# Dilated attention on one Trainium2 core: affine rows through SyncE, merges used later, a longer projection lead, and the last merge behind five evictions

## The chip, the cores and the metric

The kernel runs on one core of a Trainium2 chip. The core has a matrix engine (PE, with a separate row PEld for its weight loads), a vector engine (DVE), a scalar engine (ACT), a general engine (POOL) and a sequencer that only issues transfers (SP, also called SyncE). Each engine carries out its own list of instructions strictly in order, and they meet through semaphores. DMA transfers are issued by SP or by POOL here, in the order of that engine's list; an instruction at the head of a list that has to wait holds up everything behind it on its engine.

The metric is the device time of one execution in microseconds (us), the median of several.

## The reference

The program is a decoder trunk of two layers on 1024 tokens of width 1024, all in float32. Layer 0 mixes tokens with a gated MLP, layer 1 with dilated attention; each is followed by a squared-ReLU MLP. The change touches the attention layer only.

```python
def mixer_b(h, w_qkv, w_out, slopes):
    qkv = (h @ w_qkv).reshape(B, S, N_PAT, 3, B_HEADS, B_HEAD_DIM)
    outs, lses = [], []
    for g, (window, dilation) in enumerate(B_PATTERNS):      # (128, 1), (512, 4), (2048, 16)
        o, lse = dilated_branch(qkv[:, :, g, 0], qkv[:, :, g, 1], qkv[:, :, g, 2], window, dilation, slopes)
        outs.append(o)
        lses.append(lse)
    wts = jax.nn.softmax(jnp.stack(lses, axis=0), axis=0)[..., None]
    o = jnp.sum(wts * jnp.stack(outs, axis=0), axis=0)
    return o.reshape(B, S, B_HEADS * B_HEAD_DIM) @ w_out
...
    y = mixer_b(h, b_w_qkv[j], b_w_out[j], slopes)
    x = layer_norm(ALPHA * x + gate * y, ln_g[i, 0], ln_b[i, 0])
```

There are 16 heads of 64 and three dilations. Each dilation gives an output and a log-sum-exp; the three outputs are then mixed with softmax weights over the dilations. That mixing is called a merge below.

## The kernel before

A float32 product is made of three matmuls: each operand is split into a high part (`hi`, a cast by ACT) and a low part (`lo`, a subtraction by DVE), and hi x hi, hi x lo and lo x hi are summed. Every name that ends in `hi` or `lo` is such a part, and both are made in `split` (lines 102 and 103). So nearly every result of PE passes through ACT and then DVE before PE can use it again.

The attention stage works through 24 groups: eight pairs of heads, `hp` 0 to 7, times three dilations g = 2, 1, 0. Each group has eight slots with two half slots each. `at(slot, half)` enters a piece of work in a table; the loop at the end of `attention` runs through the slots, issues the pieces of each half slot and then one or two steps of `project()`. A step is three matmuls of 128x512 of the query and key projections of dilations 1 and 2 (`psq`, `psk`; 512 steps in all); those are spread between the attention work so that PE has something to do while DVE and ACT work on scores and probabilities. Before the first slot 44 steps are issued as a lead. From the written list a scheduler makes the order of each engine: it may move an instruction past others of its engine as long as the data allow, except for those that are given to `tc.keep_in_program_order`.

Four parts matter for the change.

*Affine rows.* The residual of the later normalisation needs ALPHA * (x * ln_g + ln_b). Eight rows of 128 tokens (`aff_0` to `aff_7`) are loaded from `spill`, multiplied by `aff_g`, increased by `aff_b` (both scaled by ALPHA on ACT), and stored back. Loads and stores are all issued by POOL. The row buffers come from `row_bc`, a ring of three buffers that the merges' `bc` use too; `aff_g` and `aff_b` hold two of them, so the rows share the third.

*Merges.* `merge(hp)` runs while the next pair is computed; its `base` is the first slot after the pair. `read` fetches the statistics, `factors` computes weights (`mm`, `ma`, `mal`: small operations of DVE and one exponential on ACT) and stores them to `w_dram` with three transfers, `spread` reads them back, broadcast over 64 partitions each, into `bc` for g = 1, 2, 0 with two transfers each, all on SP. Then twelve pieces follow on DVE: six `scale` (line 1593, output times weight), four `add` (line 1597) and two `cut` (line 103, a split). A name such as `bc_2_1` is pair 2, dilation 1; `oT_2_1` is the output of that pair and dilation, `pTlo_5_0_3` the low part of transposed probabilities of head 5, dilation 0, piece 3, `wk_4_1_lo` and `klo_3_1` the low parts of a key weight and of projected keys (pair, dilation).

*Output projection.* `accumulate` is the product with `w_out`, in parts a to e (`psoa` to `psoe` in the traces), over k = 0 to 7, one k for each pair. Parts a and b (k 0 to 3) run inside the slots of the last groups; c (second half of the tokens, rows 4 to 7, k 2 and 3) and d (first half, rows 0 to 3, k 4 to 7, which need the later merges) run after the slots, in `go_on`. Their results are added to `acc` by DVE (line 1730); a result holds one PSUM bank until that is done.

*Weights of the output projection.* `staged_unit(k, load, gate, ready)` loads rows of `w_out` (`wo_k_raw`), multiplies them by the gate on DVE and splits them into `wo_k_hi` and `wo_k_lo`. Units 6 and 7 are split late, in `go_on`.

## Time and profile before

| | us |
|---|---|
| median of three runs | 2799.32 (2795.46 to 2805.48) |
| the profiled execution | 2804.96 |
| its span in the trace | 2803.2 |
| PE busy | 2690.2 (96%) |
| PE weight loads busy | 2216.5 (79%) |
| DVE busy | 1992.5 (71%) |
| ACT busy | 1376.3 (49%) |
| POOL busy | 99.6 (4%) |

Times in the trace count from the start of the span. The attention stage with its output projection lies at about 1377 to 2155 us. In a timeline, a row gives start, duration, engine, line, operation, output and inputs, how often, and in brackets the idle time of the engine just before it with what ended it. The mean granted clock of PE was 0.983 of full over the profiled execution. A busy PE at a lower clock takes longer for the same matmuls, so both its idle time and its clock count.

### The profile page before, as it was taken

To read this page: it belongs to the slowest core of one execution; us is meant where nothing else is said; L and a number is where in the kernel's file an instruction comes from. 1 tells how busy PE (TensorE), PEld (TensorE's weight loads), DVE (VectorE), ACT (ScalarE), POOL (GpSimd) and SP (SyncE) were. 2 spreads that over 40 slices of the span, in tenths; PEclk is the share of its full clock that TensorE was granted. 3 is DMA by queue.
4 is the path that set the end of the run, shared out by engine and by line. 5 is a ranking of instruction groups with operands and counts; after the bars stand their busy time and mean duration, and the time that the engine had idled before them with its cause. 6 is when DMAs were issued, how large, how long until landed. Compare 5 with 4: busy or idle time off the path is not lost. (4 is left out here: it accounts for less than half of the span.)

```text
span 2803.2 us, 36881 instructions
## 1 busy us (share of the span) xinstructions
PE 2690.2 (96%) x13242; PEld 2216.5 (79%) x13242; DVE 1992.5 (71%) x3594; ACT 1376.3 (49%) x2593; POOL 99.6 (4%) x171
## 2 busy tenths in 40 slices
PE   6999999999999999999997999999998999999998
PEld 5787888787888788888776877777886878888887
DVE  6777697877977696656456666666667975668887
ACT  3354475555443454334344555555663755554332
POOL 1000000000000001111100000000010000000000
PEclk9999999999999999999998999999999999999999
DMA  7543347668746446655535454445574464486562
GB/s 256 161 126 121 113 152 228 214 227 284 278 155 194 154 144 225 208 197 188 177 124 167 120 142 116 117 123 151 142 195 127 162 210 151 161 283 213 170 200 88
DMA packets 332573, 487.99 MB, mean 174 GB/s; under 512 B 50988, under 2 KB 176340, under 8 KB 332388
## 3 DMA queue, kind: packets, MB, share of 16 engines
q1 hardware_dynamic: 317124, 430.04, 48.7%
q0 software_dynamic: 15264, 55.58, 5.5%
q8 instruction: 104, 1.70, 0.3%
q14 instruction: 81, 0.66, 0.1%
HBM read 357.01 MB, written 128.53 MB: 173 GB/s over the span
## 5 line engine op out<-in xcount | busy, mean ns | idle before, releaser
L796 PE MATMUL psua<-right,left 128*128 128x512 f32 x1536 | 364.9, 391 | 0.3
L955 PE MATMUL psd<-rhi,lhi 128*128 128x512 f32 x896 | 349.8, 390 | 3.0 <-ACT part L827 3.0
L955 PE MATMUL psd<-rlo,lhi 128*128 128x512 f32 x896 | 349.4, 390 | 0.2
L955 PE MATMUL psd<-rhi,llo 128*128 128x512 f32 x896 | 348.9, 389 | 0.0
L796 PEld LDWEIGHTS psua<-right,left 128*128 128x128 f32 x1536 | 288.2, 188 | 62.1 <-DVE right L103 1.4
L1447 ACT ACTIVATE p<-p,stat 128x128 f32<-128x128 f32 (+1 forms) x384 | 168.2, 439 | 127.9 <-DVE stat L1445 127.9
L955 PEld LDWEIGHTS psd<-rhi,lhi 128*128 128x128 f32 x896 | 168.5, 188 | 39.0 <-ACT part L827 3.9
L955 PEld LDWEIGHTS psd<-rlo,lhi 128*128 128x128 f32 x896 | 168.5, 188 | 35.6 <-DVE rlo L103 1.1
L955 PEld LDWEIGHTS psd<-rhi,llo 128*128 128x128 f32 x896 | 168.5, 188 | 35.2
L796 PE MATMUL psuc<-right,left 128*128 128x512 f32 x768 | 187.2, 390 | 0.0
L128 DVE SCALAR_TENSOR_TENSOR adaacc<-adaw,silu_c,adaacc 128x512 f32<-128x512 f32 x168 | 128.5, 775 | 57.9 <-DMA adaw<-in_ada_w_dram 57.2
L796 PEld LDWEIGHTS psuc<-right,left 128*128 128x128 f32 x768 | 143.5, 188 | 30.0 <-DVE right L103 0.4
L103 DVE TENSOR_TENSOR pTlo<-pT,pThi 128x512 fp32r<-128x512 f32 (+1 forms) x160 | 99.0, 620 | 65.4 <-ACT pThi L102 64.4
L103 DVE TENSOR_TENSOR left<-ws,left 128x512 fp32r<-128x512 f32 x128 | 87.8, 687 | 71.2 <-ACT left L102 69.4
L103 DVE TENSOR_TENSOR llo<-lraw,lhi 128x1024 fp32r<-128x1024 f32 x112 | 136.4, 1218 | 0.6 <-ACT lhi L102 0.6
L1345 PE MATMUL psk<-form_L,wk_hi 128*128 128x512 f32 x384 | 136.6, 435 | 0.0
L1345 PE MATMUL psq<-form_L,wq_hi 128*128 128x512 f32 x384 | 131.9, 425 | 0.0
L102 ACT CAST left<-ws 128x512 fp32r<-128x512 f32 x128 | 79.1, 620 | 99.7 <-DVE ws L717 87.7
L1445 DVE CUSTOM_DVE_ANT_0 p<-sc,bias 128x128 f32<-128x128 f32 (+1 forms) x384 | 110.1, 345 | 17.0 <-PE sc L1431 16.0
L1499 PE MATMUL pv<-pTlo,v 128*128 128x128 f32 (+1 forms) x400 | 97.3, 286 | 25.6 <-DVE pTlo L103 25.1
L1257 PE MATMUL psv<-vrhi,form_S 128*128 128x512 f32 x384 | 120.0, 390 | 0.8 <-ACT vrhi L102 0.5
L102 ACT CAST lhi<-lraw 128x1024 fp32r<-128x1024 f32 x112 | 117.4, 1048 | 3.7 <-PE psua L796 3.6
(329 smaller groups left out, 6098.6 us busy)
## 6 DMA issues: line engine op xcount, KB each, us to landing
lraw<-forms SPq DMA_DIRECT2D x112, 512.0 KB
adaw<-in_ada_w_dram SPq DMA_DIRECT2D x192, 256.0 KB
up<-in_mlp_w_up_dram SPq DMA_DIRECT2D x64, 512.0 KB
forms<-s SPq DMA_DIRECT2D x128, 256.0 KB
rraw<-in_mlp_w_down_dram SPq DMA_DIRECT2D x64, 512.0 KB
forms<-part SPq DMA_DIRECT2D x96, 256.0 KB
v<-vs POOLq DMA_DIRECT2D x48, 512.0 KB, 3.8
vraw<-in_b_w_qkv_dram SPq DMA_DIRECT2D x42, 512.0 KB
```

Source lines behind the costliest of these rows:

```text
L102: first = A.copy(hi, src) if hi_engine is A else hi_engine.tensor_copy(hi, src)
L103: return first, lo_engine.tensor_tensor(lo, src, hi, op=ALU.subtract)
L128: ins = V.scalar_tensor_tensor(acc[:], raw[:], silu_c[:, k : k + 1], acc[:], ALU.mult, ALU.add)
L796: T.matmul(acc, w[:, a, k, :], right[p][:, b, k, :], start=p in (1, 2, 5) and k + a + b == 0, stop=k == 3 and a == 1, skip_group_check=True)
L955: ins = T.matmul(sums[kind, m][:], l[a][:, k, m * P : (m + 1) * P], r[b][:, k, :], start=p in (1, 5, 2, 3) and kp + k + a + b == 0, stop=k ...
L1257: T.matmul(acc, rows[:, m * P : (m + 1) * P], cols_, start=p in (1, 2, 5) and kp + k + a + b == 0, stop=kp == 1 and k == 1 and a == 1, ski ...
L1345: T.matmul(p[:], wu[a][:, k * P : (k + 1) * P], h_op(k, half, b), start=k + c_ == 0, stop=k == KD - 1 and c_ == 2)
L1445: V.tensor_tensor_reduce(out=pr, in0=banks[e][:, sl], in1=st["bias"][:, width - w :], scale=-0.125, scalar=3e38, op0=ALU.add, op1=ALU.min, ...
L1447: A.activation(pr, pr, AF.Exp, bias=nm, scale=-1.0, accum_out=l)
L1499: T.matmul(pvs[b][:, q0 % HALF : q0 % HALF + w_], stt, x_[:, o_ : o_ + w_], start=not begun[b], stop=left[b] == 0, skip_group_check=True)
```

## The change

It has four parts, all in `attention`.

1. The affine loads are issued by SP. `aff_g`, `aff_b` and rows 0 to 3 are loaded during the lead (steps 16 to 19 of it), rows 0 to 3 into buffers of the ring `oT`; rows 4 to 7 still use `row_bc`, with the load of row i written in slot 5i - 15 and its use in slot 5i - 12. The scaling of `aff_g` and `aff_b` on ACT is a piece of its own. The loads are no longer kept in program order. The stores stay on POOL.
2. For pairs 0 to 6 `factors` and `spread` move one slot later, and the twelve pieces start at half slot 16 instead of 12, two slots later. For the last pair `spread` moves half a slot forward.
3. The lead has 48 steps instead of 44, and the remaining steps are paced evenly over all half slots.
4. The last merge's pieces are taken out of the slots. `go_on` issues part c of the output projection first and, from its sixth step on, one merge piece behind each step; then come units 6 and 7, the rest of the merge and part d. The pieces run half by half, and part d goes through k in the groups (4, 5, 6), (7) instead of in pairs. The units 4 to 7 are made ready earlier.

```diff
-                @at(*((base + 3, 0) if hp < N_PAIRS - 1 else (base + 1, 0)))
+                @at(*((base + 4, 0) if hp < N_PAIRS - 1 else (base + 1, 0)))
                 def factors():
...
-                @at(*((base + 3, 1) if hp < N_PAIRS - 1 else (base + 1, 1)))
+                @at(*((base + 4, 1) if hp < N_PAIRS - 1 else (base + 1, 0)))
                 def spread():
...
-                steps = [lambda f=f, g=g, half=half: f(g, half) for f, g in ((scale, 2), (scale, 1), (scale, 0), (add, 2), (add, 1), (cut, 0)) for half in range(2)]
+                pieces = ((scale, 2), (scale, 1), (scale, 0), (add, 2), (add, 1), (cut, 0))
+                if hp == N_PAIRS - 1:
+                    ending["merge"] = [lambda f=f, g=g, half=half: f(g, half) for half in range(2) for f, g in pieces]
+                    return
+                steps = [lambda f=f, g=g, half=half: f(g, half) for f, g in pieces for half in range(2)]
                 pace = 2 if hp < N_PAIRS - 2 else 1
                 for n, f in enumerate(steps):
-                    n = pace * n + 12 if hp < N_PAIRS - 1 else n // 2 + 8
+                    n = pace * n + 16
                     at(base + n // 2, n % 2)(f)
...
                         affine[n] = row_bc(f"aff_{n}")
-                        tc.keep_in_program_order(nc.gpsimd.dma_start(affine[n][:], src[0, 1].partition_broadcast(P)))
-                        A.mul(affine[n][:], affine[n][:], ALPHA)
-                affine["row"] = row_bc(f"aff_{i}")
-                tc.keep_in_program_order(nc.gpsimd.dma_start(affine["row"][:], spill[1][i * P : (i + 1) * P, :]))
+                        nc.sync.dma_start(affine[n][:], src[0, 1].partition_broadcast(P))
+                t = affine[i] = vec.tile([P, S], F32, name=f"aff_{i}", tag="oT", bufs=4) if i < 4 else row_bc(f"aff_{i}")
+                nc.sync.dma_start(t[:], spill[1][i * P : (i + 1) * P, :])
+
+            def affine_scale():
+                for n in "gb":
+                    A.mul(affine[n][:], affine[n][:], ALPHA)
             def affine_row(i):
-                t = affine["row"]
+                t = affine[i]
                 for n, op in (("g", ALU.mult), ("b", ALU.add)):
...
+            at(0, 0)(affine_scale)
             for i in range(NT):
-                at(2 + 3 * i, 0)(lambda i=i: affine_load(i))
-                at(3 + 3 * i, 1)(lambda i=i: affine_row(i))
+                if i > 3:
+                    at(5 * i - 15, 0)(lambda i=i: affine_load(i))
+                at(*((i + 1, 1) if i < 4 else (5 * i - 12, 1)))(lambda i=i: affine_row(i))
...
             staged_unit(3, (-10, 1), (-9, 1), (-8, 0))
-            staged_unit(4, (-2, 0), (2, 0), (12, 0))
-            staged_unit(5, (-1, 0), (4, 0), (12, 1))
-            late = [staged_unit(6, (13, 0), (14, 1), None), staged_unit(7, (13, 1), (15, 1), None)]
+            staged_unit(4, (-2, 0), (2, 0), (8, 0))
+            staged_unit(5, (-1, 0), (4, 0), (8, 1))
+            late = [staged_unit(6, (9, 0), (11, 1), None), staged_unit(7, (9, 1), (12, 1), None)]
...
                     sums = {key: bank("mm", f"pso{name}_{key[0]}_{key[1]}") for key in groups}
-                    todo = [ks[n : n + 2] for n in range(0, len(ks), 2)]
+                    todo = ks if side > 1 else [ks[n : n + 2] for n in range(0, len(ks), 2)]
                     for pair in todo:
...
                                     T.matmul(sums[i, dh][:], ending["oT"][half][a][:, k, o : o + P], ending["units"][k][b][:, w],
-                                             start=k == ks[0] and a + b == 0, stop=k == ks[-1] and a == 1)
+                                             start=k == todo[0][0] and a + b == 0, stop=k == todo[-1][-1] and a == 1)
                             if pair is not todo[-1]:
...
             def go_on():
+                steps = ending["merge"]
+                for n, _ in enumerate(accumulate(1, range(2, 4), name="c")):
+                    if n > 4:
+                        steps.pop(0)()
                 for f in late:
                     f()
-                run(accumulate(1, range(2, 4), name="c"))
-                run(accumulate(0, range(4, 8), last=True, side=2, name="d"))
+                for f in steps:
+                    f()
+                run(accumulate(0, ((4, 5, 6), (7,)), last=True, side=2, name="d"))
...
             stream = project()
-            for _ in range(5 * KD + 4):
+            lead, credit = 6 * KD, 0
+            for n in range(lead):
                 next(stream)
+                if 16 <= n < 20:
+                    affine_load(n - 16)
             due = 0
...
                         f()
-                    for _ in range(2 if (2 * n + half) % 3 == 2 else 1):
+                    credit += 512 - lead
+                    while credit >= 351:
+                        credit -= 351
                         next(stream, None)
                     if n >= last_group - 8:
-                        due += 5 if n < last_group + 5 else 7 if n < last_group + 10 else 4
+                        due += 6
                         while due >= 8:
```

How this moves instructions shows in the order of each engine. The first place is ACT at the start of the stage. `psq` and `psk` are projections in PSUM, `qs` belongs to the values phase before, `vpart` are evictions of that phase. Before:

```order
L102 COPY wk_0_1_hi_11406<-wk_0_1_raw_11404 128x1024
L102 COPY qs_1_3_3_11221<-vpart_0_1_6_3_11003 128x512
L102 COPY qhi_0_2_11286<-psq_0_2_1_11288 128x16x32
L1634 ACTIVATE aff_g_11532<-aff_g_11532 128x1024
L1634 ACTIVATE aff_b_11535<-aff_b_11535 128x1024
L102 COPY qhi_0_2_11286<-psq_0_2_0_11315 128x16x32
L102 COPY wq_1_2_hi_11522<-wq_1_2_raw_11520 128x1024
L102 COPY khi_0_2_11348<-psk_0_2_1_11350 128x16x32
```

After, at the place of the same `qhi_0_2`:

```order
L102 COPY qhi_0_2_11286<-psq_0_2_1_11288 128x16x32
L102 COPY wq_1_2_hi_11533<-wq_1_2_raw_11531 128x1024
L102 COPY qhi_0_2_11286<-psq_0_2_0_11315 128x16x32
L102 COPY khi_0_2_11348<-psk_0_2_1_11350 128x16x32
L102 COPY wk_1_2_hi_11658<-wk_1_2_raw_11656 128x1024
```

and `aff_g` earlier, in the values phase:

```order
L102 COPY form_S1_8494<-l21_3_8437 128x512
L1219 COPY vpart_0_1_6_0_10946<-psv1_0_1_0_10703 128x512
L1643 ACTIVATE aff_g_11354<-aff_g_11354 128x1024
L1219 COPY vpart_0_1_6_1_10964<-psv1_0_1_1_10720 128x512
L1219 COPY vpart_0_1_6_2_10985<-psv1_0_1_2_10739 128x512
```

The two scalings (`aff_g`, `aff_b`) stood between the two halves of `qhi_0_2`; now `aff_g` stands some 25 rows earlier between two evictions `vpart`, and `aff_b` likewise a few rows behind it.

The second place is DVE at merge 2, behind the eight score reductions of `sc_6_2_1` and `sc_7_2_1`. Before:

```order
L1593 TENSOR_TENSOR bc_2_1_14377<-oT_2_1_13969,bc_2_1_14377 128x512
L103 TENSOR_TENSOR klo_3_1_14308<-psk_3_1_1_14309,khi_3_1_14307 128x4x128
L103 TENSOR_TENSOR pTlo_5_0_3_14454<-pT_5_0_3_14449,pThi_5_0_3_14453 128x384
L1509 TENSOR_TENSOR oT_2_0_14317<-oT_2_0_14317,pv_5_0_1_14341 64x512
L1593 TENSOR_TENSOR bc_2_2_14380<-oT_2_2_13664,bc_2_2_14380 128x512
L103 TENSOR_TENSOR pTlo_6_2_0_14492<-pT_6_2_0_14486,pThi_6_2_0_14491 128x512
L1593 TENSOR_TENSOR bc_2_2_14380<-oT_2_2_13664,bc_2_2_14380 128x512
L103 TENSOR_TENSOR wk_4_1_lo_14989<-wk_4_1_raw_14986,wk_4_1_hi_14988 128x1024
L103 TENSOR_TENSOR klo_3_1_14308<-psk_3_1_0_14457,khi_3_1_14307 128x4x128
L1509 TENSOR_TENSOR oT_3_2_14610<-oT_3_2_14610,pv_6_2_0_14520 64x512
```

After:

```order
L103 TENSOR_TENSOR pTlo_5_0_3_14452<-pT_5_0_3_14447,pThi_5_0_3_14451 128x384
L1509 TENSOR_TENSOR oT_2_0_14323<-oT_2_0_14323,pv_5_0_1_14347 64x512
L103 TENSOR_TENSOR pTlo_6_2_0_14497<-pT_6_2_0_14491,pThi_6_2_0_14496 128x512
L1593 TENSOR_TENSOR bc_2_2_14458<-oT_2_2_13674,bc_2_2_14458 128x512
L103 TENSOR_TENSOR wk_4_1_lo_14981<-wk_4_1_raw_14978,wk_4_1_hi_14980 128x1024
L103 TENSOR_TENSOR klo_3_1_14283<-psk_3_1_0_14440,khi_3_1_14282 128x4x128
L1509 TENSOR_TENSOR oT_3_2_14616<-oT_3_2_14616,pv_6_2_0_14524 64x512
...
L103 TENSOR_TENSOR pTlo_6_2_1_14584<-pT_6_2_1_14578,pThi_6_2_1_14583 128x512
L1593 TENSOR_TENSOR bc_2_2_14458<-oT_2_2_13674,bc_2_2_14458 128x512
L103 TENSOR_TENSOR qlo_4_2_14512<-psq_4_2_1_14513,qhi_4_2_14511 128x16x32
L1593 TENSOR_TENSOR bc_2_1_14455<-oT_2_1_13971,bc_2_1_14455 128x512
```

The first scale was `bc_2_1`, ahead of `klo`, `pTlo` and `oT`. Now it is `bc_2_2`, behind two `pTlo` and `oT` and ahead of `wk_4_1_lo` and the second half of `klo_3_1` (`psk_3_1_0`).

The third place is DVE after the last slots, where the last merge meets the evictions `acc` of part c. Before:

```order
L1572 TENSOR_TENSOR ma_7_19069<-ma_7_19069,mal_7_19074 128x16 x3
L103 TENSOR_TENSOR pTlo_15_0_2_19039<-pT_15_0_2_19033,pThi_15_0_2_19038 128x512
L1509 TENSOR_TENSOR oT_7_0_19005<-oT_7_0_19005,pv_15_0_0_19027 64x512
L103 TENSOR_TENSOR pTlo_15_0_3_19063<-pT_15_0_3_19058,pThi_15_0_3_19062 128x384
L1509 TENSOR_TENSOR oT_7_0_19005<-oT_7_0_19005,pv_15_0_1_19028 64x512
L1593 TENSOR_TENSOR bc_7_1_19097<-oT_7_1_18721,bc_7_1_19097 128x512 x2
L1730 TENSOR_TENSOR acc_2_4_18886<-acc_2_4_18886,psoc_4_0_19165 128x512
L1730 TENSOR_TENSOR acc_2_4_18886<-acc_2_4_18886,psoc_4_1_19166 128x512
L1593 TENSOR_TENSOR bc_7_2_19100<-oT_7_2_18425,bc_7_2_19100 128x512 x2
L103 TENSOR_TENSOR wo_4_lo_19117<-wo_4_raw_18591,wo_4_hi_19116 128x1024
L103 TENSOR_TENSOR wo_5_lo_19123<-wo_5_raw_18615,wo_5_hi_19122 128x1024
```

After:

```order
L103 TENSOR_TENSOR pTlo_15_0_3_19079<-pT_15_0_3_19074,pThi_15_0_3_19078 128x384
L1572 TENSOR_TENSOR ma_7_19085<-ma_7_19085,mal_7_19090 128x16 x3
L1509 TENSOR_TENSOR oT_7_0_19031<-oT_7_0_19031,pv_15_0_0_19049 64x512
...
L1739 TENSOR_TENSOR acc_2_5_18874<-acc_2_5_18874,psoc_5_0_19159 128x512
L1739 TENSOR_TENSOR acc_2_5_18874<-acc_2_5_18874,psoc_5_1_19160 128x512
L1593 TENSOR_TENSOR bc_7_1_19101<-oT_7_1_18743,bc_7_1_19101 128x512
L1739 TENSOR_TENSOR acc_2_6_18931<-acc_2_6_18931,psoc_6_0_19175 128x512
L1593 TENSOR_TENSOR bc_7_1_19101<-oT_7_1_18743,bc_7_1_19101 128x512
...
L1593 TENSOR_TENSOR bc_7_0_19107<-oT_7_0_19031,bc_7_0_19107 128x512
L103 TENSOR_TENSOR wo_6_lo_19211<-wo_6_raw_19110,wo_6_hi_19210 128x1024
L103 TENSOR_TENSOR wo_7_lo_19215<-wo_7_raw_19116,wo_7_hi_19214 128x1024
```

The scales stood ahead of the first `acc`; now four `acc` (4 and 5, the last two of them shown) stand ahead of the first scale, and the last operation of `factors` (`ma_7`) has moved behind `pTlo_15_0_3`.

## The prediction

> **What bounds the kernel now.** The page was read first. Over the whole program the matrix engine (PE) works nearly all the time, so only the stretches where it stands still or runs slowly can be won. The view by windows shows where those lie in the attention stage; its columns are the stretch, then the busy time of PE, its weight loads, DVE, ACT and POOL, then the granted PE clock, the DMA share and GB/s.
>
> ```profile
> core 0 of [0], span 2803.2 us
> 1377.00:1560.00 183.00, 157.68 (x871) 129.07 (x870) 95.54 (x254) 76.84 (x219) 15.57 (x31) 0.91 0.50 153
> 1560.00:2000.00 440.00, 421.31 (x2744) 351.43 (x2744) 289.10 (x884) 259.11 (x772) 11.78 (x32) 0.98 0.48 129
> 2000.00:2155.00 155.00, 140.79 (x796) 115.35 (x795) 106.46 (x275) 78.96 (x197) 10.16 (x14) 0.93 0.66 177
> ```
>
> PE is idle for 183.0 - 157.68 = 25.3 us in the opening, 18.7 in the middle and 14.2 at the end: 58.2 us. The granted clock costs more: (1 - PEclk) times the busy time is 14.2 + 8.4 + 9.9 = 32.5 us. About 91 us is all that these stages can give.
>
> The timeline of PE names the stalls; in brackets stands the idle time before a row and what ended it.
>
> ```profile
> 1404.43 0.79 PE L1345 MATMUL psk<-form_S,wk_hi 128*128 128x512 f32 x1 [6.87 <-DVE qlo L103]
> ...
> 1454.91 0.33 PE L1499 MATMUL pv<-pThi,v 128*128 128x128 f32 x1 [1.59 <-ACT pThi L102]
> ...
> 1480.21 0.39 PE L1499 MATMUL pv<-pThi,v 128*128 128x256 f32 x1 [3.98 <-ACT pThi L102]
> ...
> 1510.45 0.58 PE L1499 MATMUL pv<-pTlo,v 128*128 128x256 f32 x1 [8.34 <-DVE pTlo L103]
> ...
> 1543.40 0.47 PE L1431 MATMUL sc<-klo,qhi 64*128 64x128 f32 x2 [2.38 <-DVE klo L103]
> ...
> 1702.01 0.39 PE L1499 MATMUL pv<-pTlo,v 128*128 128x256 f32 x1 [2.27 <-DVE pTlo L103]
> ...
> 1709.94 0.33 PE L1431 MATMUL sc<-klo,qhi 64*128 64x128 f32 x2 [0.97 <-DVE klo L103]
> ...
> 1783.95 0.39 PE L1499 MATMUL pv<-pTlo,v 128*128 128x256 f32 x1 [2.17 <-DVE pTlo L103]
> ...
> 2111.12 0.79 PE L1717 MATMUL psoc<-wo_hi,oTs 128*128 128x512 f32 x1 [4.07 <-DVE acc L1730]
> ...
> 2120.13 0.80 PE L1717 MATMUL psoc<-wo_hi,oTs 128*128 128x512 f32 x1 [3.62 <-DVE acc L1730]
> ...
> 2124.30 0.47 PE L1717 MATMUL psod<-wo_hi,oTs 128*128 128x512 f32 x1 [1.24 <-DVE acc L1730]
> ```
>
> All of them wait for DVE or ACT, though neither is busy enough to be the bound. What holds those two is taken up part by part below. Around each stall the clock falls:
>
> ```profile
> 1397.00:1417.00 20.00, 13.13 (x47) 10.28 (x46) 6.71 (x7) 5.55 (x7) 1.07 (x2) 0.83 0.79 273
> 1440.00:1460.00 20.00, 17.30 (x103) 13.36 (x103) 12.07 (x33) 8.66 (x27) 2.21 (x4) 0.94 0.37 132
> 1480.00:1500.00 20.00, 19.37 (x119) 16.12 (x120) 13.04 (x32) 11.45 (x31) 1.63 (x3) 0.91 0.60 177
> 1500.00:1520.00 20.00, 11.66 (x60) 9.97 (x59) 8.62 (x31) 6.41 (x25) 1.69 (x4) 0.66 0.40 125
> 1540.00:1560.00 20.00, 17.60 (x97) 14.52 (x97) 12.65 (x34) 7.82 (x26) 0.00 (x0) 0.83 0.28 79
> 1682.00:1722.00 40.00, 36.71 (x223) 30.60 (x223) 25.82 (x89) 22.45 (x72) 0.77 (x2) 0.96 0.38 95
> 2100.00:2120.00 20.00, 12.45 (x45) 9.31 (x43) 12.28 (x17) 3.66 (x5) 0.84 (x1) 0.82 0.69 168
> 2120.00:2140.00 20.00, 18.63 (x75) 14.70 (x76) 15.75 (x34) 5.48 (x8) 0.00 (x0) 0.92 0.40 129
> ```
>
> With the same product, the clock costs 2.2 us at the opening (0.17 x 13.13), 1.0, 1.7 and 4.0 around the first head pair, 3.0 at the first merge, 1.5 at a later merge, 2.2 and 1.5 at the end.
>
> **A. Affine loads, start of attention.** ACT's queue shows what the 6.87 us stall waited for.
>
> ```profile
> 1391.86 0.60 POOL L1633 DMA_DIRECT2D aff_g<-in_ln_g_dram  x1 [2.82 <-DMA wk_raw<-in_b_w_qkv_dram]
> 1400.52 1.06 ACT L1634 ACTIVATE aff_g<-aff_g 128x1024 f32<-128x1024 f32 x1 [12.65 <-DMA aff_g<-in_ln_g_dram]
> ...
> 1341.00:1361.00 20.00, 20.00 (x90) 16.57 (x89) 8.92 (x12) 7.69 (x11) 2.90 (x6) 1.00 0.25 89
> ```
>
> ACT sat 12.65 us before scaling `aff_g`, which landed 1400.52 - 1391.86 = 8.66 us after POOL issued it. Behind it in ACT's order stands the `qhi` eviction, behind that DVE's `qlo`, behind that a PSUM bank for PE. The change issues this load on SP, ahead of the projection lead, and the order of ACT shows the scaling now between two evictions of the values phase, near 1341 us, and `aff_b`'s near 1353. So A is worth 6.87 + 2.2 = 9.1 us. What hides the two new waits is the bank and form backlog there: in 1341 to 1361 PE is busy 20.00 of 20 us while ACT works 7.69, and the DMA share is 0.25 against 0.79 or more around the old place. If that cover is gone, each wait is at most the 8.66 us of the old landing less some 3 us between issue and use in the order, 5.7 us, twice: 11 us, more than A's gain. The DMA load and the ample idle time of ACT are nearest to no wait; I take 9.1 gained, with +2 lost to -9.1 as the ends. On SP the four early row loads stand ahead of `wq_0_1_raw` and its successors and the first waits for a PE step near 1360; the weights behind it are wanted some 20 us later, so nothing is charged.
>
> **B. Affine rows in the first head pair.** The chain of one row through one buffer is seen here (the store of a row, the load of the next, the multiply that waits for it):
>
> ```profile
> 1491.38 0.54 POOL L1642 DMA_DIRECT2D spill<-aff  x1 [10.09 <-DVE aff L1641]
> ...
> 1497.90 0.54 POOL L1636 DMA_DIRECT2D aff<-spill  x1 [5.99 <-DMA spill<-aff]
> ...
> 1505.80 1.23 DVE L1641 TENSOR_TENSOR aff<-aff,aff_g 128x1024 f32<-128x1024 f32 x1 [8.65 <-DMA aff<-spill]
> ```
>
> Store issue to next multiply took 1505.80 - 1491.38 = 14.4 us, with DVE standing 8.65 us at the head of its queue, and `pTlo`, for which PE waited 8.34 us, behind it. The three stalls sum to 1.59 + 3.98 + 8.34 = 13.9, their clock to 1.0 + 1.7 + 4.0 = 6.7: 20.6 us. After the change rows 0 to 3 have buffers of their own and are loaded before the stage, row 4 too; DVE multiplies them with nothing to wait for. The multiplies themselves (two of some 1.2 us a row) are the same in number. Rows 5, 6 and 7 still wait for the store of the row before. Between that store and their multiply the order leaves some 11.4 to 12.5 us of other work, where the longest chain shown took 14.4: at most 3 us left at one or two of them. B's ends are 20.6 and, if all three wait 3 us with the clock of a small stall (1.0 each), 8.6; the loads no longer queue with stores on POOL, so I take 2.5 left and 18.1 gained.
>
> **C. Merges 0 to 6.** A merge computes weights on DVE, stores them through `w_dram` and reads them back spread over partitions (`bc`), two transfers for each of three dilations. The rows are SP's and DVE's, first of merge 2, then of merge 6:
>
> ```profile
> 1692.71 0.36 SPq L1574 DMA_DIRECT2D w_dram<-ma  x1
> 1694.79 0.48 SPq L1581 DMA_DIRECT2D bc<-w_dram  x1
> ...
> 1699.86 1.03 DVE L1593 TENSOR_TENSOR bc<-oT,bc 128x512 f32<-128x512 f32 x1 [3.83 <-DMA bc<-w_dram]
> ...
> 1708.06 1.22 DVE L103 TENSOR_TENSOR wk_lo<-wk_raw,wk_hi 128x1024 fp32r<-128x1024 f32 x1 [1.38 <-ACT wk_hi L102]
> 1709.20 0.68 DVE L103 TENSOR_TENSOR klo<-psk,khi 128x512 fp32r<-128x512 f32 x1
> ...
> 2022.86 0.48 SPq L1581 DMA_DIRECT2D bc<-w_dram  x1
> ...
> 2030.56 1.03 DVE L1593 TENSOR_TENSOR bc<-oT,bc 128x512 f32<-128x512 f32 x1 [1.23 <-DMA bc<-w_dram]
> ```
>
> The first pair of `bc` is usable 5.07 us after the first issue (1694.79 to 1699.86), the second 7.70 us after it (2022.86 to 2030.56). DVE stood 3.83 us at the first scale, with `pTlo` behind it, and PE lost 2.27 there and 0.97 more at `klo`. A merge costs 3.24 idle + 1.5 clock = 4.7 us; merges 1 to 5 carry 5 x 3.24 = 16.2 of the middle's 18.7 idle. Merge 0 costs 2.38 + 3.0 = 5.4.
>
> The change puts the factors one slot later and their first use two slots later in the written list: one slot more room, which is 3.4 us (two merges are 24 slots and 1783.95 - 1702.01 = 81.9 us apart), nearly the 3.83 of the wait. The order of DVE says otherwise: in merge 2 the first scale is now that of `bc_2_2`, the *second* pair, so it wants 2.6 us more than before. The factors end about 3 us later, near 1695.8; the first issue follows 2.0 later as before, 1697.8; the second pair is usable at 1705.5. Three of DVE's operations, `pTlo`, `oT`, `pTlo`, moved ahead of the scale, so PE's 2.27 us wait goes; DVE comes to the scale near 1702.5 and stands 3.0 us. But queued behind it now are the scale (1.03), `wk_lo` (1.22) and the second half of `klo` (0.68), ready near 1708.4. PE came to that `klo` at 1709.94 - 0.97 = 1708.97 after losing 2.27 and some 1.5 of clock, so without those it comes at 1705.2 and waits 3.2 us: the idle time of before in one piece instead of two. With its clock (1.5 to 3) I charge 0.7 us more at each of merges 2 to 5. In merges 0 and 1 `klo` stands ahead of the scale and only some 1.7 us of stall and 1 of clock is left: 2.7 gained at merge 0, 2.0 at merge 1. Merge 6 moves by under 2 us in either direction, taken as nothing. C is 4 x 0.7 - 4.7, about -2. Its ends: if the second pair lands as the first does (5.07), 2.6 us less wait in each and no clock, -23; if it is late by those 2.6 us once more, 2.6 lost in each of six merges, +16. The value is nearest to the 7.70 row, the only one that shows a second pair.
>
> Lead of 48 steps and the even pacing: no matmul is added; 512 steps stay 512. Four steps of three matmuls, some 2.7 us of PE work, move from the pairs' middle to the lead, which the loads of the weights must cover 2.7 us sooner. It gives `klo`'s eviction that much more time at first and nothing at the end, and stands in the `klo` estimate; charged at 0.
>
> Which stalls cost clock decides what one long stall in place of two is worth. Here 2.27 and 0.97 us of idle already brought the clock to 0.96 over 40 us. The Trainium skill, page "TensorE: Matmul & The Clock Gate", section "Why this matters for your kernels", warns only of idle gaps above some 3 us between bursts of matmuls; the trace disagrees with that bound. By the skill's bound the merges' short stalls cost no clock before and the new 3.2 us ones would, and the sum would be some 9 us worse (a rival, below).
>
> **D. The last merge.** Four rows carry it:
>
> ```profile
> 2095.95 0.35 DVE L1572 TENSOR_TENSOR ma<-ma,mal 128x16 f32<-128x16 f32 x3
> ...
> 2098.91 0.56 DVE L103 TENSOR_TENSOR pTlo<-pT,pThi 128x384 fp32r<-128x384 f32 x1
> ...
> 2108.38 1.03 DVE L1593 TENSOR_TENSOR bc<-oT,bc 128x512 f32<-128x512 f32 x1 [6.86 <-DMA bc<-w_dram]
> ...
> L1717 PE MATMUL psod<-wo_hi,oTs x64: 387/389/469, 2124.3 to 2146.0; 128*128 128x512 f32 x64
> ```
>
> DVE stood 6.86 us at the first `bc`, two scales ahead of the evictions of `psoc`, and PE lost 4.07 + 3.62 + 1.24 = 8.9 us plus 3.7 of clock: 12.6. The order now has four evictions ahead of the first scale and one after each of the next, so `psoc`, whose end made way for `psod` at 2124.30 - 1.24 = 2123.1, can end some 11 us earlier, near 2112 (7.7 of stall and some 3 of clock). Two things are late next. The last factor operation moved behind `pTlo_15_0_3`: 2098.91 against 2095.95, so the `bc` land some 3 us later, near 2111.4. And `psod` now does k = 4, 5, 6 of a group at once, so PE meets `wo_6_lo` after two of those k (1.4 us); it stands on DVE behind a scale of the third pair, near 2120. From there the rest of `psod`'s 96 matmuls (21.7 us, 2124.3 to 2146.0 before) ends near 2141. Gain 5 us. Ends: 12.6 if the weights come in time, 0 if the `bc` are another 5 us late.
>
> **Sum.** -9.1 - 18.1 - 2 - 5 = -34, and 1 us for the two waits in the values phase that I cannot exclude: -33. The profiled execution took 2804.96 us, 5.6 over the median of 2799.32; off the median this makes 2766 us.
>
> **Rivals.** *Everything lands in time*: C -23, D -12.6, B -20.6, A -9.1 give -65, 2734 us. For it speaks the one slot that the list adds; against it the second pair's 7.70 us.
> *The waits move with the loads*: ACT stands in the values phase for most of A (+8), and rows 5 to 7 keep 8 us; -33 + 8 + 6 = -19, 2780 us. The 8.66 us landing speaks for it, PE's full 20.00 us with a DMA share of 0.25 against.
> *Slower, by one mechanism*: the scale of `bc_2_*` at merges 2 to 5, with `klo` behind it on DVE. Each us that the second pair lands later costs PE a us at four merges. To cancel the other -33 it must be 33 / 4 = 8.3 us later, usable 16 us after the first issue; to be slower by over 0.3%, 10.4 later. A landing 12 later would give 2814. The largest delay in the rows is 3 us, so this is unlikely.
> *Short stalls are free, long ones are not*: if the fall to 0.96 had another cause than merge 2's own short stalls, the merges had no clock to win, and four new stalls of 3.2 us cost 2.2 each: 4 x 2.2 = +9, about 2775 us. The stall of 1.59 us at 1454.91, in a window at 0.94, speaks against it. (It is the Trainium skill's clock bound, named above.)
>
> **How the numbers follow.** Forecast 0.62, all in time 0.13, waits move 0.14, slower 0.06, short stalls free 0.05. The forecast's own bounds are C's, A's and D's: 2750 to 2784. The range takes in most of the rivals on both sides: 2743 to 2786. A measurement here can tell about 0.3%, 8.4 us: slower has 0.06, a like time 0.04 (the end of the third case), faster 0.90.
>
> **What would show it.** A: no stall of PE over 1 us between 1380 and 1415, ACT's `aff_g` scaling before 1350. B: no `aff` row of DVE with more than 3 us of idle. C: the idle time before the first `bc` scale still about 3 us at merges 2 to 5, and a PE stall on `klo` of 3 to 4 us in place of the pair. D: `psoc` without stalls, one stall of `psod` on `wo_lo` of some 5 us. The prediction is wrong if the stalls on `klo` are gone or beyond 8 us, or if ACT stands in the values phase with PE waiting.

## The result and the profile after

| | before | after |
|---|---|---|
| median, us | 2800.95 (2795.46 to 2805.48, 4 runs) | 2758.04 (2755.41 to 2763.34, 4 runs) |
| profiled execution, us | 2804.96 | 2759.17 |
| its span, us | 2803.2 | 2757.5 |

The ratio is 0.985 (95% interval 0.9826 to 0.9874): 42.9 us less by the medians. The forecast was 2766, 33 less, with a range of 2743 to 2786.

The page of the changed kernel, its first lines, and the view by windows (columns as in the prediction):

```profile
span 2757.5 us, 36894 instructions
PE 2678.4 (97%) x13242; PEld 2206.1 (80%) x13242; DVE 1991.9 (72%) x3594; ACT 1375.1 (50%) x2593; POOL 96.3 (3%) x161
```

```profile
1377.00:1417.00 40.00, 40.00 (x195) 33.02 (x194) 20.49 (x38) 13.76 (x28) 4.49 (x8) 1.00 0.82 252
1377.00:1560.00 183.00, 178.93 (x1102) 147.73 (x1101) 120.69 (x326) 98.46 (x286) 14.04 (x26) 1.00 0.58 167
1560.00:2000.00 440.00, 423.11 (x2742) 350.55 (x2741) 292.78 (x894) 256.34 (x765) 12.88 (x32) 0.98 0.50 134
2000.00:2155.00 155.00, 147.84 (x781) 120.38 (x780) 122.21 (x291) 95.73 (x200) 8.21 (x10) 0.98 0.53 149
```

In the first 40 us of the stage PE is busy 40.00 of 40 us at full clock, where it lost 6.87 us and some clock before. The opening to 1560 has 4.1 us of idle in place of 25.3 and a clock of 1.00 in place of 0.91. The middle has hardly changed: 16.9 us idle in place of 18.7, at 0.98 as before (the same 440 us now hold later work). The end has 7.2 idle and 0.98 in place of 14.2 and 0.93.

What is left is in PE's timeline (the klo stalls of merges 2 and 4, the `pThi` stall of merge 3, and the two at the end):

```profile
1669.63 0.33 PE L1431 MATMUL sc<-klo,qhi 64*128 64x128 f32 x2 [1.86 <-DVE klo L103]
...
1743.45 0.39 PE L1499 MATMUL pv<-pThi,v 128*128 128x256 f32 x1 [1.71 <-ACT pThi L102]
...
1833.14 0.33 PE L1431 MATMUL sc<-klo,qhi 64*128 64x128 f32 x2 [2.04 <-DVE klo L103]
...
2057.53 0.45 PE L1499 MATMUL pv<-pThi,v 128*128 128x256 f32 x2 [2.43 <-ACT pThi L102]
...
2080.07 0.50 PE L1726 MATMUL psod<-wo_lo,oTs 128*128 128x512 f32 x1 [0.66 <-DVE wo_lo L103]
```

DVE's groups show the waits for transfers. The last column is the idle time before each group; in the kernel before it was 14.6 us for the first and 28.8 for the second, 24.9 of that for transfers.

```profile
L1648 DVE TENSOR_TENSOR aff<-aff,aff_g 128x1024 f32<-128x1024 f32 x8 | 9.7, 1216 | 0.0
...
L1593 DVE TENSOR_TENSOR bc<-oT,bc 128x512 f32<-128x512 f32 x48 | 44.2, 940 | 9.1 <-DMA bc<-w_dram 9.0
```

By stretches of the two profiled executions the difference of the spans, 45.7 us, lies as follows. A pair's start is POOL's score bias for its dilation 2; the rows of pairs 2 and 6 are shown, of the kernel before and then of the changed one.

```profile
1593.85 0.67 POOL L1419 TENSOR_SCALAR bias<-far 128x128 f32<-128x128 f32 x2 [27.87 <-DVE stat L1445]
...
1921.37 0.68 POOL L1419 TENSOR_SCALAR bias<-far 128x128 f32<-128x128 f32 x2 [27.77 <-DVE stat L1445]
```

```profile
1558.48 0.67 POOL L1419 TENSOR_SCALAR bias<-far 128x128 f32<-128x128 f32 x2 [27.14 <-DVE stat L1445]
...
1881.55 0.67 POOL L1419 TENSOR_SCALAR bias<-far 128x128 f32<-128x128 f32 x2 [27.79 <-DVE stat L1445]
```

| stretch | before | after | difference |
|---|---|---|---|
| start to the first `psq` matmul | 1381.1 | 1378.9 | -2.2 |
| from there to pair 1 (parts A and B) | 128.4 | 99.8 | -28.6 |
| pairs 1 to 2 (holds merge 0) | 84.3 | 79.8 | -4.6 |
| pairs 2 to 3 (merge 1) | 81.8 | 79.0 | -2.8 |
| pairs 3 to 7 (merges 2 to 5) | 326.6 | 325.0 | -1.7 |
| pair 7 to the first `psoe` matmul | 144.0 | 135.5 | -8.4 |
| from there to the end | 656.9 | 659.5 | +2.6 |

The last stretch lies outside of what the change touches, and the first holds only its early affine loads and two scalings. Profiled executions differ there by as much: over all kernels below, the first `psq` comes at 1374.5 to 1382.8 us and the last stretch takes 655.9 to 659.9.

### The profile page after: what moved, and what is told of

It reads as the page before. It is cut to its first block, busy times and chain, and to the rows that moved or that the text cites. A ratio compares the mean times of both kernels' runs of the same rounds, so it can differ in the third digit from the quotient of the medians.

```text
span 2757.5 us, 36894 instructions
## 1 busy us (share of the span) xinstructions
PE 2678.4 (97%) x13242; PEld 2206.1 (80%) x13242; DVE 1991.9 (72%) x3594; ACT 1375.1 (50%) x2593; POOL 96.3 (3%) x161
## 5 line engine op out<-in xcount | busy, mean ns | idle before, releaser
L128 DVE SCALAR_TENSOR_TENSOR adaacc<-adaw,silu_c,adaacc 128x512 f32<-128x512 f32 x168 | 128.4, 774 | 54.0 <-DMA adaw<-in_ada_w_dram 53.5
L1345 PE MATMUL psk<-form_L,wk_hi 128*128 128x512 f32 x384 | 130.3, 418 | 0.0
L102 ACT CAST rhi<-rraw 128x1024 fp32r<-128x1024 f32 x48 | 50.6, 1053 | 139.6 <-issue 113.8
```

Source lines behind the costliest of these rows:

```text
L102: first = A.copy(hi, src) if hi_engine is A else hi_engine.tensor_copy(hi, src)
L128: ins = V.scalar_tensor_tensor(acc[:], raw[:], silu_c[:, k : k + 1], acc[:], ALU.mult, ALU.add)
L1345: T.matmul(p[:], wu[a][:, k * P : (k + 1) * P], h_op(k, half, b), start=k + c_ == 0, stop=k == KD - 1 and c_ == 2)
```

## The experiments

The medians of the kernel before in the three groups of runs were 2799.5, 2799.6 and 2800.9 us, so the medians below can be set side by side within some 2 us. Below, a difference to the kernel before is worked out from the ratio, and one to the changed kernel from the medians.

| run | median, us | ratio to before (95% interval) | pair 2 to pair 6, us |
|---|---|---|---|
| before | 2800.95 | 1 | 327.5 |
| the change | 2758.04 | 0.985 (0.9826 to 0.9874) | 323.1 |
| e14, the change once more | 2758.94 | 0.9852 (0.9828 to 0.9876) | 323.5 |
| e1, affine part alone | 2769.23 | 0.9899 (0.9882 to 0.9915) | 324.9 |
| e5, merges alone | 2782.84 | 0.9948 (0.9931 to 0.9964) | 314.0 |
| e6, lead alone | 2792.03 | 0.9976 (0.9964 to 0.9988) | 319.8 |
| e7, the change with the old end | 2762.90 | 0.9871 (0.9857 to 0.9886) | 326.3 |
| e2, the change with loads on POOL | 2770.63 | 0.9899 (0.9881 to 0.9916) | 326.8 |
| e3, the change with bc in order 2, 1, 0 | 2757.00 | 0.9855 (0.9833 to 0.9877) | 323.3 |
| e9, the change with the old lead | 2748.55 | 0.9821 (0.9804 to 0.9838) | 317.1 |
| e10, the change with the old pacing of the output steps | 2759.15 | 0.9856 (0.9836 to 0.9875) | 322.9 |
| e12, the change with scales half a slot later | 2744.80 | 0.9799 (0.9773 to 0.9825) | 313.3 |
| e13, e12 with the old lead | 2752.40 | 0.9827 (0.9805 to 0.9849) | 318.6 |

### e1: the affine part alone

The kernel before with part 1 of the change; its lead keeps 44 steps.

```diff
-            for _ in range(5 * KD + 4):
+            for n in range(5 * KD + 4):
                 next(stream)
+                if 16 <= n < 20:
+                    affine_load(n - 16)
...
+                        nc.sync.dma_start(affine[n][:], src[0, 1].partition_broadcast(P))
+                t = affine[i] = vec.tile([P, S], F32, name=f"aff_{i}", tag="oT", bufs=4) if i < 4 else row_bc(f"aff_{i}")
+                nc.sync.dma_start(t[:], spill[1][i * P : (i + 1) * P, :])
```

> The kernel before with only the affine part of the change (loads on SyncE, aff_g, aff_b and rows 0 to 3 in the lead, own buffers, new slots). Theory (the stalls of the opening are the affine waits and nothing else): parts A and B of the prediction in full, -27 to -31 us against before, no PE stall over 2 us before the first merge at some 1530 us; the merges keep their pair of stalls of 2.2 and 1.0 us. Rival (the longer lead gives part of the opening): -20 us at most, a PE stall of 2 us or more stays between 1400 and 1515.

Measured: 0.9899, 28.3 us less, the theory's. No PE stall over 1 us is left before the first merge, and the merges keep their pairs of stalls, here those of merge 1:

```profile
1586.78 0.39 PE L1499 MATMUL pv<-pTlo,v 128*128 128x256 f32 x1 [2.27 <-DVE pTlo L103]
...
1594.68 0.33 PE L1431 MATMUL sc<-klo,qhi 64*128 64x128 f32 x2 [0.95 <-DVE klo L103]
```

So A and B together are the affine waits, and they are worth some 28 us with the old lead (e1) as with the new one (28.6 in the stretch that holds them, above).

### e5: the merges alone

```diff
-                @at(*((base + 3, 0) if hp < N_PAIRS - 1 else (base + 1, 0)))
+                @at(*((base + 4, 0) if hp < N_PAIRS - 1 else (base + 1, 0)))
                 def factors():
...
-                @at(*((base + 3, 1) if hp < N_PAIRS - 1 else (base + 1, 1)))
+                @at(*((base + 4, 1) if hp < N_PAIRS - 1 else (base + 1, 1)))
                 def spread():
...
-                    n = pace * n + 12 if hp < N_PAIRS - 1 else n // 2 + 8
+                    n = pace * n + 16 if hp < N_PAIRS - 1 else n // 2 + 8
```

> The kernel before with only the merges of pairs 0 to 6 moved (factors and spread one slot later, pieces two slots later). Theory (the two slots buy time at all merges, some of it lost again to the second pair in front of klo): -5 to -9 us, one stall on klo of about 2 us at each of merges 2 to 5 in place of the pair of 2.2 and 1.0. Prediction's step C as it stood: about -2 us with a klo stall of 3.2 us. Rival (without the longer lead klo comes no sooner, and the extra slots alone bring nothing): 0 us, klo stalls of 3 us or more.

Measured: 0.9948, 14.6 us less, more than either expected. One stall on `klo` is left at each merge, and it is small; DVE's wait for the second pair and PE's wait at merge 2, and the middle stretch:

```profile
1702.48 1.11 DVE L1593 TENSOR_TENSOR bc<-oT,bc 128x512 f32<-128x512 f32 x1 [0.59 <-DMA bc<-w_dram]
...
1705.38 0.33 PE L1431 MATMUL sc<-klo,qhi 64*128 64x128 f32 x2 [1.01 <-DVE klo L103]
...
1560.00:2000.00 440.00, 429.28 (x2857) 359.63 (x2856) 301.80 (x923) 270.14 (x805) 12.38 (x34) 1.00 0.50 134
```

The klo stalls of merges 1 to 5 are 1.01 to 1.35 us, and the clock stays at 1.00 over 440 us (other stalls of this length did cost clock, as the rivals at the end show). From pair 2 to pair 6 it takes 314.0 us, 3.4 less a pair than before. In the change the same four pairs take 323.1. So the change gives most of the merges' gain back.

### e6: the lead alone

```diff
-            for _ in range(5 * KD + 4):
+            lead, credit = 6 * KD, 0
+            for n in range(lead):
                 next(stream)
...
-                    for _ in range(2 if (2 * n + half) % 3 == 2 else 1):
+                    credit += 512 - lead
+                    while credit >= 351:
+                        credit -= 351
                         next(stream, None)
```

> The kernel before with only the lead of 48 steps and the even pacing. Theory (no work added or hidden by itself; the waits of the affine rows and merges stand where they stood): 0 us, within 3 us. Rival (the lead is what shortens the klo stalls): -4 to -8 us, with the stall of 0.97 us on klo gone at merges 1 to 5.

Measured: 0.9976, 6.7 us less, the rival's. The klo stalls of merges 1 to 4 are gone; the wait at `pTlo` stays, and so does the opening:

```profile
1400.34 1.22 PE L1345 MATMUL psk<-form_S,wk_hi 128*128 128x512 f32 x2 [7.73 <-DVE qlo L103]
...
1696.36 0.39 PE L1499 MATMUL pv<-pTlo,v 128*128 128x256 f32 x1 [1.52 <-DVE pTlo L103]
```

The prediction had charged the lead at nothing.

### e9: the change with the lead and pacing of before

The diff of e6 taken back in the changed kernel.

> The changed kernel with the lead of 44 steps and the pacing of before. Theory (with the longer lead PE runs out of projection steps ahead of the scores and meets klo earlier, its stall passes some 1.5 us and the clock falls): -6 to -10 us against the changed kernel, merges 78.4 us apart instead of some 81, as with the merges alone. Rival (the merges alone gained because the opening was late, and the longer lead helps): +3 us or more.

Measured: 0.9821, 9.5 us less than the change by the medians. The pairs are 79.3 us apart, not quite the 78.5 of the merges alone. At merge 2 the klo stall is 1.38 us where the change has 1.86:

```profile
1667.87 0.33 PE L1431 MATMUL sc<-klo,qhi 64*128 64x128 f32 x2 [1.38 <-DVE klo L103]
...
1560.00:2000.00 440.00, 425.48 (x2794) 355.04 (x2793) 302.29 (x921) 264.65 (x789) 13.87 (x33) 0.99 0.51 143
```

So the same edit gains 6.7 us on the kernel before and loses 9.5 in the change. This is why the parts do not add up: 28.3, 14.6, 6.7 and some 5 (e7, below) would be 55, and together they give 43. Without the lead they nearly do: 28.3, 14.6 and 5 are 48, and e9 is 50 less than the kernel before.

### e3: the pair that is needed first comes first

```diff
-                    for g in (1, 2, 0):
+                    for g in (2, 1, 0):
                         bc = box[g] = row_bc(f"bc_{hp}_{g}")
```

> The changed kernel with the six bc transfers issued for dilation 2 first (2, 1, 0 instead of 1, 2, 0), so that the first scale needs the first pair. Theory (the wait for the second pair in front of klo is what merges 2 to 5 still lose): DVE's wait at the first scale gone, klo stalls of PE from 1.9 to 2.1 us down to under 1 and the clock of the middle at 1.00: -6 to -10 us against the changed kernel, near 2750. Rival (the klo stalls come from wk_lo and the projection's position, not from the bc wait): within 2 us of the changed kernel.

Measured: 0.9855, the time of the change and so the rival's number, though the klo stall fell, at merge 2 to 0.48 us. The scheduler, with the first pair ready sooner, put the scale two places earlier on DVE, ahead of `oT` and `pTlo`, and DVE stands there for 3.05 us:

```profile
1663.93 1.09 DVE L1593 TENSOR_TENSOR bc<-oT,bc 128x512 f32<-128x512 f32 x1 [3.05 <-DMA bc<-w_dram]
...
1666.53 0.33 PE L1499 MATMUL pv<-pTlo,v 128*128 128x128 f32 x1 [1.02 <-DVE pTlo L103]
...
1668.26 0.33 PE L1431 MATMUL sc<-klo,qhi 64*128 64x128 f32 x2 [0.48 <-DVE klo L103]
```

At merge 2 a part of the wait moved from `klo` to `pTlo`. The edit also changed the order, so the experiment does not decide what the wait in front of `klo` costs.

### e12 and e13: the scale behind `klo`

e12 is the change with its merge pieces half a slot later; e13 is e12 with the lead and pacing of before.

```diff
-                    n = pace * n + 16
+                    n = pace * n + 17
```

> The changed kernel (lead of 48 steps) with the merge pieces half a slot later (17 in place of 16), so that on DVE the first scale stands behind the second half of klo. Theory (what merges 2 to 5 still lose is klo waiting behind the scale that waits for bc): the klo stalls of 1.9 to 2.1 us go, the clock of the middle rises to 0.99 or 1.00, -5 to -10 us against the changed kernel, about 2750. Rival (with the longer lead PE runs out of other work there whatever DVE's order): klo or pTlo stalls of 1.5 us and more stay, within 3 us of the changed kernel.

> The changed kernel with the lead and pacing of before and the merge pieces half a slot later. Theory: the klo stalls of 1.0 to 1.4 us that were left with the old lead go too: -3 to -8 us against that kernel (2748.6), near 2743. Rival (those stalls cost no clock and something else waits in their place): 2747 to 2750.

> The changed kernel itself once more, on the chip of the two others: 2756 to 2760, so that differences of 3 us can be read; merges 2 to 5 again some 81 us apart if their stalls are of the program and not of chance. If the merges' spacing moves by 2 us between two profiles, the klo stalls and clock falls are partly chance.

Measured: e12 0.9799, 14.1 us less than the change on the same chip (e14: 2758.94), more than expected, and the fastest kernel of this study. At merge 2 the second half of `klo` now stands ahead of a scale that still waits, PE has no stall there, and the pairs are 78.3 us apart.

```profile
1662.10 0.68 DVE L103 TENSOR_TENSOR klo<-psk,khi 128x512 fp32r<-128x512 f32 x1
1663.90 0.69 DVE L1593 TENSOR_TENSOR bc<-oT,bc 128x512 f32<-128x512 f32 x1 [1.11 <-DMA bc<-w_dram]
...
1560.00:2000.00 440.00, 426.51 (x2794) 354.34 (x2794) 306.29 (x925) 265.70 (x792) 14.38 (x33) 0.99 0.53 145
```

Of the 14 us, 9.8 lie between pairs 2 and 6 (323.1 to 313.3; 10.2 against e14), which hold four merges. So what the merges still lost in the change hung on the place of the merge pieces; that it was `klo` behind the first scale fits the rows, but all twelve pieces moved and no run moves that scale alone.

e13 took 2752.40 us, 7.6 more than e12 and no better than e9 (2748.55), which misses the theory and lies just above the rival's 2747 to 2750. With the old lead a klo stall of 0.97 us remains at every merge, though `klo` now stands ahead of the scale:

```profile
1666.83 0.33 PE L1431 MATMUL sc<-klo,qhi 64*128 64x128 f32 x2 [0.97 <-DVE klo L103]
```

The lead is thus worth -6.7 us on the kernel before, +9.5 in the change, and -7.6 with the scale behind `klo`. DVE's rows show what it does where it gains. In front of `klo` stands `wk_lo`, and with the old lead, where no scale ahead of it has held DVE up longer, `wk_lo` waits for ACT's `wk_hi`: 1.57 or 1.58 us at merges 0 to 5 of e13, and 1.38 at merge 2 of the kernel before (the row at 1708.06 in the prediction). With the longer lead the wait at merge 2 is 0.26 us in e12 and none in e6. The rows are of e13 and then of e6:

```profile
1664.95 1.23 DVE L103 TENSOR_TENSOR wk_lo<-wk_raw,wk_hi 128x1024 fp32r<-128x1024 f32 x1 [1.58 <-ACT wk_hi L102]
```

```profile
1700.03 1.22 DVE L103 TENSOR_TENSOR wk_lo<-wk_raw,wk_hi 128x1024 fp32r<-128x1024 f32 x1
```

In e12 the wait is back at merges 3 to 5 (0.88 to 1.67 us), with a klo stall of 0.99 at one of them. In the change and in e9 `wk_lo` of merge 2 comes right behind a scale that has waited for its transfer, and waits for nothing, so there an earlier `wk_hi` gains nothing.

Why the longer lead costs time in the change is only partly seen. At its merge 2 `klo` is ready 12.0 us after the last factor (1657.59 to 1669.58) and PE comes to it after 10.2; with the merges alone it is 11.6 and 10.7. That is 0.9 us of stall a merge, of the 2.3 that a pair takes longer; the rest goes with the clock, 0.98 against 1.00 (PE is busy 77.9 us a pair against 76.4).

e14 repeated the change: the klo stalls of merges 2 to 5 were 1.78, 1.64, 1.34 and 2.09 us (1.86, none, 2.04 and 2.06 in the first profile; merge 3 had one of 1.71 on `pThi` in both). So the stalls are of the program, but single ones differ by 0.7 us, or by being there or not, from one execution to the next.

### e2: the affine loads on POOL again

```diff
-                        nc.sync.dma_start(affine[n][:], src[0, 1].partition_broadcast(P))
+                        nc.gpsimd.dma_start(affine[n][:], src[0, 1].partition_broadcast(P))
...
-                nc.sync.dma_start(t[:], spill[1][i * P : (i + 1) * P, :])
+                nc.gpsimd.dma_start(t[:], spill[1][i * P : (i + 1) * P, :])
```

> The changed kernel, its affine loads issued by POOL again, at the same places of the written list and with the same buffers. Theory (early issue and own buffers do it, the queue is of no matter): within 3 us of the changed kernel, some -40 us against before, no stall of PE over 2 us between 1380 and 1515. Rival (SyncE's queue as such is faster, and on POOL the loads stand behind the stores again): +8 us or more against the changed kernel, with DVE's aff rows waiting for DMA.

Measured: 0.9899, 12.6 us more than the change: the rival's number, though not by its mechanism. Only one `aff` row waits for a transfer, for 0.84 us. The row loads now stand between the `qk` stores of the values phase on POOL's queue, and DVE's `qlo` waits for a `qk` store:

```profile
1365.85 1.17 POOL L1639 DMA_DIRECT2D aff<-spill  x2
...
1395.14 0.69 DVE L103 TENSOR_TENSOR qlo<-psq,qhi 128x512 fp32r<-128x512 f32 x1 [3.54 <-DMA qk<-qs]
...
1395.89 0.74 PE L1345 MATMUL psk<-form_L,wk_hi 128*128 128x512 f32 x2 [2.92 <-DVE qlo L103]
```

From the first `psq` to pair 1 it took 104.7 us against 99.8, so some 5 of the 12 us are seen at this place. That the loads ahead of it delayed the store is likely and not shown; between 1340 and 1400 us the stores landed after 4.7 us (median), against 4.2 in the change. Of the rest, 3 us lie ahead of the first `psq`, no more than that stretch varies by, and the others behind the start of pair 1, where the edit touches only the last `aff` row; they stay unexplained.

### e7 and e10: the end

e7 puts the last merge, the units 4 to 7, part d and the pacing of the output steps back as before; e10 only the pacing.

```diff
-                        due += 6
+                        due += 5 if n < last_group + 5 else 7 if n < last_group + 10 else 4
```

> The changed kernel with the last merge, the units 4 to 7 and part d of the output projection put back as before. Theory (D is worth the stalls of psoc and their clock, some 9 to 12 us): +8 to +12 us against the changed kernel, some -32 against before, with psoc stalls of about 4 and 3.6 us back. The prediction's D: +5. Rival (the gain at the end came from the earlier merges being late no more, not from the new order): +2 or less.

> The changed kernel with the pacing of the output projection's steps of before (5, 7, 4 eighths in place of 6). Theory (with 6 the steps of part b are used up before the last probabilities, so PE waits 2.4 us for pThi behind ACT's exponential of the last merge, and the clock falls behind it): that stall is covered, -3 to -6 us against the changed kernel. Rival (the wait is given back in psoc and psod, whose weights and bc come no sooner): within 2 us.

e7 measured 0.9871: 4.9 us more than the change by the medians, 6 by the ratios. The prediction had 5, the theory 8 to 12. The old stalls are back (its `psoc` at 2067.74 and 2076.74):

```profile
2067.74 0.79 PE L1723 MATMUL psoc<-wo_hi,oTs 128*128 128x512 f32 x1 [5.56 <-DVE acc L1736]
...
2076.74 0.80 PE L1723 MATMUL psoc<-wo_hi,oTs 128*128 128x512 f32 x1 [4.26 <-DVE acc L1736]
```

The whole times hide a part of it. From pair 7 to the first `psoe`, the stretch that holds the end and merge 6, e7 took 145.7 us, and the change 135.5 (137.5 in e14): 8 to 10 more. Its start up to the first `psq`, which the edit does not touch, happened to be 4.4 us shorter than the change's. So the end is worth 5 to 6 us by whole times and 8 to 10 by its stretch, and these runs do not settle which. The stalls of e7, 9.8 us and 1.2 at `psod`, are more than the end gains, since the new end has waits of its own: 2.43 us at 2057.53 and 0.87 behind it. In the changed kernel DVE and ACT show what they hang on:

```profile
2055.22 0.17 DVE L1560 TENSOR_TENSOR mm<-mst 128x16 f32<-128x16 f32 x1 [1.94 <-DMA mst<-st_dram]
...
2056.02 0.24 ACT L1565 ACTIVATE ma<-ma 128x48 f32<-128x48 f32 x1 [2.08 <-DVE ma L1564]
...
2071.78 1.10 DVE L1593 TENSOR_TENSOR bc<-oT,bc 128x512 f32<-128x512 f32 x1 [1.16 <-DMA bc<-w_dram]
```

The statistics of the last pair arrive late for the factors, ACT's exponential stands 2.08 us, and `pThi` behind it. e10 covers this wait with steps of part b, and the stall is gone, but `psoc` then waits 4.96 us and the time is the change's (0.9856):

```profile
2071.12 0.80 PE L1726 MATMUL psoc<-wo_hi,oTs 128*128 128x512 f32 x1 [4.96 <-DVE acc L1739]
```

So the rival held: here the wait that was covered in one place was paid in the next.

## Why the prediction was right

The time fell inside the range, 8 us below the forecast, and the waits that carry A, B and C were found where the prediction had them. C was mis-sized, the lead was put at nothing and is not, and D came out near its number with other waits inside.

- *A and B*, predicted 9.1 and 18.1 less 1, together -26: measured -28.6 in the profile, -28.3 alone (e1). The two waits in the values phase are there but hidden: ACT stood 1.51 us for `aff_g` and PE lost nothing.

```profile
1340.39 1.06 ACT L1643 ACTIVATE aff_g<-aff_g 128x1024 f32<-128x1024 f32 x1 [1.51 <-DMA aff_g<-in_ln_g_dram]
```

  Of the 2.5 us left over for rows 5 to 7, nothing showed: no `aff` row waited. That the issuing queue as such matters was not predicted; e2 shows a part of it.
- *C*, predicted -2: this term was mis-sized. By the pairs' spacing C and the lead together are about -9: -4.6 and -2.8 at merges 0 and 1 (predicted -2.7 and -2.0), -1.7 at merges 2 to 5 (predicted +2.8). The mechanism was right, DVE waiting at the second pair with `klo` behind it. DVE's rows at merge 2 (the last factor, the scale of the second pair, `klo`) and SP's first `bc` issue:

```profile
1657.24 0.35 DVE L1572 TENSOR_TENSOR ma<-ma,mal 128x16 f32<-128x16 f32 x3
...
1666.79 1.05 DVE L1593 TENSOR_TENSOR bc<-oT,bc 128x512 f32<-128x512 f32 x1 [1.50 <-DMA bc<-w_dram]
...
1668.90 0.68 DVE L103 TENSOR_TENSOR klo<-psk,khi 128x512 fp32r<-128x512 f32 x1
```

```profile
1659.59 3.67 SPq L1581 DMA_DIRECT2D bc<-w_dram  x6
```

  The second pair was usable 7.20 us after the first issue (predicted 7.70), 9.2 us behind the last factor. The failed step is when DVE comes there: the prediction put it 6.7 us behind the last factor and the wait at 3.0. It was 7.7 and 1.5, because `pTlo` and `oT` on the way wait for ACT themselves. The klo stall became 1.86 and not 3.2. That the merges still cost clock was right in sum: the middle stays at 0.98. (The end of +16 that the prediction gives for C is six times 2.6 us; counted from its -2 it would be some +14.)
- *The lead*, predicted 0: wrong, and hidden in C. Alone it gives -6.7, in the change it costs 9.5 (e6, e9). That the sum came as near as it did is partly luck, since two errors cancel: from pair 1 to pair 7 the kernel before takes 492.8 us, the change with the old lead 475.0 (e9) and the change 483.8. So without the lead C would be some -18 (the merges alone, e5, have 474.0) where the prediction had -2, and the lead gave half of that back.
- *D*, predicted -5: -5 to -6 by whole times (e7), -8 by its stretch in the two profiles. The inside was different: `psoc` ran without a stall as foreseen, but `psod` waited only 0.66 us for `wo_lo` in place of some 5, and 3.3 us went to `pThi` and `pTlo` behind the late statistics, which the prediction had not seen.
- *The rivals.* All in time would be 2734; e12 comes to 2744.8 with most of the merges' waits off the path and the end unchanged. The rival by which short stalls cost no clock is answered by single stalls. In e13 the klo stall of merge 4, 0.97 us long, has 4 us at a clock of 0.62 behind it. In e9 the one of merge 2, 1.38 us long (its row at 1667.87 above), has 4 us at 1.00 behind it. The rows are of e13 and then of e9:

```profile
1825.67 0.33 PE L1431 MATMUL sc<-klo,qhi 64*128 64x128 f32 x2 [0.97 <-DVE klo L103]
...
1827.00:1831.00 4.00, 4.00 (x14) 3.25 (x15) 2.98 (x14) 3.22 (x13) 0.00 (x0) 0.62 0.61 156
```

```profile
1669.00:1673.00 4.00, 4.00 (x20) 3.06 (x19) 1.62 (x12) 3.16 (x13) 0.00 (x0) 1.00 0.51 141
```

  So a stall of 1 us can cost clock, and the length of a stall alone does not say whether it does. The Trainium skill, in "TensorE: Matmul & The Clock Gate", section "Why this matters for your kernels", warns of idle gaps above some 3 us between bursts of matmuls. Here the clock fell behind a stall well below that, the 0.97 us of e13.

## What to carry to other kernels

Where a wait for a transfer stands in an engine's order, ask which work is queued behind it and when that work is wanted. Here half a slot more for the waiting work, which put one small operation (`klo`) ahead of it, came with 14 us on top of the two slots that the change had given it. Then ask what that operation waits for next: with the old lead the same edit gained nothing, because `wk_hi` was late there. An edit that gains alone (a longer lead) can cost as much beside another, so parts that share a queue are to be measured together and apart. When a transfer is made to arrive sooner, read the order again, since a scheduler may put its user sooner too.

## What was not expected of the hardware

The clock did not follow the length of PE's stalls. With klo stalls of 1.01 to 1.35 us at merges 1 to 5 it stayed at 1.00 over 440 us (e5), and in e1 it was 1.00 in a pair with stalls of 2.40 and 1.13 us (from 1804.54 to 1885.24). It was 0.98 in a pair of e13 whose longest stall was 0.97 us (from 1794.23 to 1874.84), and in each of the three pairs from 3 to 6 in both profiles of the change, with stalls of 1.3 to 2.1 us. What decides it is not shown here. Issuing the same ten affine loads on SyncE and not on POOL was worth 12.6 us with the same buffers and places in the list (e2), of which 5 could be placed.
